# A depthwise convolution's taps in pairs, spread over three attention heads, and pooling one head ahead

## The chip, the cores and the metric

The kernel runs on one core of a Trainium2 chip. The metric is the time of one execution on the device in microseconds. The kernel before took 2637.24 us in the median of three runs (2633.56 to 2638.14).

## The reference, cut to what matters

Two networks of transformer blocks run one after the other on 512 latent tokens (x) and 256 context tokens, width 1024. The first network has two blocks, the second one. Only the mixing part of the first network's two blocks is touched. Each of these has three branches whose outputs are joined and projected: differential attention with 4 heads, a pooling of four window lengths, and a gated depthwise convolution over 31 tokens with a normalization behind it.

```python
for l in range(2):                     # the first network's two blocks
    ...
    attn = diff_attn_post(diff_attention(q, k_all, v_all, lam), subln_g[l], lambda_init)
    pool_o = pool_mixer(up, pool_w[l], pool_scale[l])
    conv_o = conformer_conv(ca, cb, conv_dw_w[l], conv_dw_b[l], conv_ln_g[l], conv_ln_b[l])
    mix = jnp.concatenate([attn, pool_o, conv_o], axis=-1)
    x = x + g1 * jnp.einsum('blm,md->bld', mix, w_out[l])
    ...                                # the first block does the same for the context tokens

def diff_attention(...):               # per 128 queries and head: two score maps
    p = jax.nn.softmax(s, axis=-1)
    a = p[:, :, 0] - lam * p[:, :, 1]  # the combination
    return jnp.einsum('bhqk,bhkd->bhqd', a.astype(v_all.dtype), v_all)

def multiscale_pool(u):                # mean of 2, 4, 8 or 16 neighbours, minus u
    ...
def conformer_conv(a, b, dw_w, dw_b, ln_g, ln_b):
    u = a * jax.nn.sigmoid(b)
    y = lax.conv_general_dilated(u, dw_w[:, None, :], ...)   # 31 taps on 256 channels
    return jax.nn.silu(layer_norm(y + dw_b, ln_g, ln_b))
```

## The kernel before

Activations lie with channels on the 128 partitions. Weights come in pieces of 512 KB by the SyncE queue and are split into a high and a low part, the high part on ScalarE (line 229), the low part on GpSimd (line 230); a projection is three matmuls for each product (lines 254, 257, 258).

**Attention.** `attn` goes through the four heads, and in each through query tiles of 128 rows: 6 tiles in the first block (two of the context, with 256 keys, and four latent ones with 768), 4 in the second. A tile's scores are matmuls into two PSUM tiles (line 836; the pool has two of them, so the next tile's scores wait until this tile's exponentials have read them). VectorE takes the row maximum (line 799), ScalarE the exponential (803), VectorE the reciprocal and lambda's factor (841 to 843) and the *combination* of the two maps (844). `attn_values`, for the tile before, transposes the combined map on TensorE (815), copies it on ScalarE (817), multiplies with the values (819), and normalizes with a power on GpSimd (297, tile `ray`) and two products on VectorE (860, 862); `turn` transposes the result (867).

**Work beside the heads.** `windows` returns five lists of items: one for the time before head 0, and one for each head, of which `layer` issues a share after each tile. Items are projections (`q1` and so on: each head's queries and keys are projected a head ahead, normalized on VectorE and GpSimd in `qk_norm`, lines 759 to 782, and turned on TensorE, 791), modulation columns (`m`), taps (`t`), pooling (`pool`), and the convolution's normalization (`ln`). An item's later stages wait in a list until enough matmul time has been issued.

**Convolution.** `conv_taps` runs on VectorE. There are 2 channel tiles (ct) of 31 taps each; a tap is one instruction over the whole token range (783 columns in the first block, 512 in the second) that multiplies a shifted view of `uc[ct]` by a column and adds it to the output tile `mix[6 + ct]` (line 664; the first one, with the bias, is line 662). Items hold four taps. Seven items stand in head 0's list and nine in head 1's. They are issued with a priority lowered by 1500 places. `conv_ln` (lines 671 to 690) takes means by a matmul with ones (676) and normalizes.

**Pooling.** `pool_mix` adds shifted views on GpSimd (line 614), two or four adds for each segment, into two scratch tiles, which are the convolution's inputs `uc`; so it can begin only when the taps have read these. VectorE does edges and the mean minus u (lines 639 to 644), a matmul the weights (649). Its two items stand in head 2's list, with the normalization.

**What sets the order.** The code is recorded in this order, and a scheduler then places instructions on each engine by priority (the place in the recording, raised or lowered by `high_priority`) along a timeline of its own. On the chip each engine runs its own list in that order, and waits by semaphores where it needs another engine's result.

## Time and profile before

| | us |
|---|---|
| median of 3 runs (lowest, highest) | 2637.24 (2633.56, 2638.14) |
| the profiled execution | 2634.79 |
| its span, first to last instruction | 2632.9 |
| TensorE busy | 2500.2 (95%) |
| VectorE busy | 954.6 (36%) |
| ScalarE busy | 907.7 (34%) |
| GpSimd busy | 1143.8 (43%) |

The busy shares are of the whole span, and the change touches two stretches of it: the attention of the first block, about 80 to 385 us, and that of the second, about 1100 to 1340 us. In the profile PE is TensorE, DVE VectorE, ACT ScalarE, POOL GpSimd. The granted clock of TensorE is given as a share of 2.4 GHz; at its lower level it is 1.2 GHz, so a stretch in which it is low for a fifth of the time shows 0.9. Times in views by time are from the span's start.

### The profile page before, as it was taken

To read this page: it belongs to the slowest core of one execution; us is meant where nothing else is said; L and a number is where in the kernel's file an instruction comes from. 1 tells how busy PE (TensorE), PEld (TensorE's weight loads), DVE (VectorE), ACT (ScalarE), POOL (GpSimd) and SP (SyncE) were. 2 spreads that over 40 slices of the span, in tenths; PEclk is the share of its full clock that TensorE was granted. 3 is DMA by queue.
4 is the path that set the end of the run, shared out by engine and by line. 5 is a ranking of instruction groups with operands and counts; after the bars stand their busy time and mean duration, and the time that the engine had idled before them with its cause. 6 is when DMAs were issued, how large, how long until landed. Compare 5 with 4: busy or idle time off the path is not lost.

```text
span 2632.9 us, 38646 instructions
## 1 busy us (share of the span) xinstructions
PE 2500.2 (95%) x15840; PEld 2131.1 (81%) x15840; DVE 954.6 (36%) x1932; ACT 907.7 (34%) x1905; POOL 1143.8 (43%) x965
## 2 busy tenths in 40 slices
PE   7889989999999999999999999999998898999998
PEld 5778869988888889877788777778887788888887
DVE  4896464121120123488542112113322756210112
ACT  4334543322122124333534223234443543422222
POOL 4544324433333334655326545454322344555553
PEclk9889989999999999999999999999998999999999
DMA  7113311323323233222324435343111021222221
GB/s 253 50 49 110 116 72 40 121 81 113 96 96 102 91 99 101 78 65 81 97 80 145 160 128 160 120 160 104 49 33 51 17 97 49 81 96 97 96 92 53
DMA packets 68961, 248.55 MB, mean 94 GB/s; under 512 B 7472, under 2 KB 10800, under 8 KB 67120
## 3 DMA queue, kind: packets, MB, share of 16 engines
q1 hardware_dynamic: 64992, 231.11, 26.9%
q10 hardware_dynamic: 3792, 14.97, 1.5%
q8 instruction: 125, 2.05, 0.3%
q14 instruction: 52, 0.43, 0.0%
HBM read 239.75 MB, written 6.29 MB: 93 GB/s over the span
## 4 chain that ended last, share of the span: by engine, by line
PE 48%; DVE 5%; ACT 2%; POOL 2%; issue 1%; DMA 1%; POOLq 0%; DVEq 0%; ACTq 0%
PE s2t L254 6%; PE s2t L258 6%; PE s2t L257 6%; PE pj L254 5%; PE pj L257 5%; PE pj L258 5%; PE ap L819 2%; DVE mix L664 1%; PE ap L254 1%; PE ap L257 1%; PE ap L258 1%; POOL wlo L230 1%; PE s2t L1531 1%; PE s2t L836 1%; PE ap L343 1%
## 5 line engine op out<-in xcount | busy, mean ns | idle before, releaser
L230 POOL TENSOR_TENSOR wlo<-raw,whi 128x512 fp32r<-128x512 f32 x576 | 745.4, 1326 | 700.5 <-ACT whi L229 700.2
L229 ACT CAST whi<-raw 128x512 fp32r<-128x512 f32 x576 | 319.5, 615 | 675.2 <-PE pj L257 248.1
L254 PE MATMUL s2t<-hh,whi 128*128 128x512 f32 (+1 forms) x1184 | 448.9, 380 | 0.8 <-ACT whi L229 0.8
L257 PE MATMUL s2t<-hl,whi 128*128 128x512 f32 (+1 forms) x1184 | 446.2, 377 | 1.8 <-POOL hl L428 1.8
L258 PE MATMUL s2t<-hh,wlo 128*128 128x512 f32 (+1 forms) x1184 | 447.5, 378 | 0.1
L254 PE MATMUL pj<-hh,whi 128*128 128x256 f32 (+1 forms) x1088 | 337.2, 312 | 8.5 <-ACT hh L425 2.9
L257 PE MATMUL pj<-hl,whi 128*128 128x256 f32 (+1 forms) x1088 | 331.5, 305 | 3.5 <-DVE hl L430 2.4
L258 PE MATMUL pj<-hh,wlo 128*128 128x256 f32 (+1 forms) x1088 | 331.1, 305 | 0.3 <-POOL wlo L230 0.3
L954 DVE TENSOR_TENSOR sg<-sg,s2t 128x512 f32<-128x512 f32 x66 | 45.4, 688 | 651.8 <-ACT sg L953 651.8
L257 PEld LDWEIGHTS s2t<-hl,whi 128*128 128x128 f32 x1184 | 223.0, 189 | 47.0 <-POOL hl L428 2.9
L258 PEld LDWEIGHTS s2t<-hh,wlo 128*128 128x128 f32 x1184 | 223.1, 188 | 46.9 <-issue 1.2
L254 PEld LDWEIGHTS s2t<-hh,whi 128*128 128x128 f32 x1184 | 222.4, 188 | 46.3 <-issue 2.1
L254 PEld LDWEIGHTS pj<-hh,whi 128*128 128x128 f32 x1088 | 210.4, 194 | 25.1 <-ACT hh L425 4.0
L327 POOL TENSOR_TENSOR gl<-sg,gh 128x512 fp32r<-128x512 f32 (+1 forms) x66 | 97.7, 1481 | 293.4 <-ACT gh L326 293.4
L257 PEld LDWEIGHTS pj<-hl,whi 128*128 128x128 f32 x1088 | 211.0, 194 | 12.4 <-DVE hl L430 2.6
L258 PEld LDWEIGHTS pj<-hh,wlo 128*128 128x128 f32 x1088 | 209.6, 193 | 8.5 <-POOL wlo L230 0.5
L254 PE MATMUL pj<-whi,hh 128*128 128x256 f32 x672 | 196.9, 293 | 1.3 <-ACT v L699 0.9
L257 PE MATMUL pj<-wlo,hh 128*128 128x256 f32 x672 | 194.4, 289 | 0.0
L258 PE MATMUL pj<-whi,hl 128*128 128x256 f32 x672 | 193.9, 289 | 0.0
L893 DVE SCALAR_TENSOR_TENSOR xt<-pj,mod,xt 128x256 f32<-128x256 f32 x224 | 101.6, 480 | 175.6 <-PE pj L258 175.1
L258 PE MATMUL pj<-gh,wlo 128*128 128x512 f32 (+1 forms) x400 | 145.6, 364 | 0.0
L254 PE MATMUL pj<-gh,whi 128*128 128x512 f32 (+1 forms) x400 | 145.5, 366 | 0.0
(382 smaller groups left out, 4464.7 us busy)
## 6 DMA issues: line engine op xcount, KB each, us to landing
raw<-in_w_mod SPq DMA_DIRECT2D x144, 512.0 KB, 4.0
raw<-in_w_up SPq DMA_DIRECT2D x132, 512.0 KB, 3.9
raw<-in_w_dn SPq DMA_DIRECT2D x66, 512.0 KB, 4.0
raw<-in_w_in SPq DMA_DIRECT2D x60, 512.0 KB, 3.9
raw<-in_w_out SPq DMA_DIRECT2D x24, 512.0 KB, 3.9
xt<-xs ACTq DMA_DIRECT2D x4, 1024.0 KB, 5.7
xt<-in_xT ACTq DMA_DIRECT2D x2, 1024.0 KB, 7.9
xs<-xt SPq DMA_DIRECT2D x2, 1024.0 KB, 3.8
```

Source lines behind the costliest of these rows:

```text
L229: nc.scalar.copy(out=h, in_=raw[:, q])
L230: nc.gpsimd.tensor_tensor(out=lo[:, s][:, q], in0=raw[:, q], in1=h.bitcast(F32), op=ALU.subtract)
L254: i = mm(ps, lhsT=lh, rhs=rh, start=start, stop=False)
L257: mm(ps, lhsT=lh, rhs=rl, start=False, stop=False)
L258: return mm(ps, lhsT=ll, rhs=rh, start=False, stop=stop)
L327: (lo_eng or self.nc.vector).tensor_tensor(out=lo, in0=src, in1=hi.bitcast(F32), op=ALU.subtract)
L343: nc.tensor.matmul(ps[g:g + 32], lhsT=self.cond_t[:, k, :], rhs=raw[k // 4][:, k % 4, :], start=k < 4, stop=k >= 4, tile_position=(0, g))
L664: nc.vector.scalar_tensor_tensor(out=m, in0=u[:, j:j + W], scalar=dw(j), in1=m, op0=ALU.mult, op1=ALU.add)
L819: i = nc.tensor.matmul(o, lhsT=at[:, j], rhs=v[:, j0 + j, :], start=j0 + j == 0, stop=j0 + j == nj - 1)
L836: nc.tensor.matmul(s[c][:, k0:k1], lhsT=qk[r, 0, a, t], rhs=qk[r, 1, b, k0:k1], start=n == 0, stop=n == 2)
L893: self.nc.vector.scalar_tensor_tensor(out=x, in0=ps, scalar=col, in1=x, op0=ALU.mult, op1=ALU.add)
L954: nc.vector.tensor_tensor(out=sg[:, c], in0=sg[:, c], in1=p[:, 1], op=ALU.mult)
```

## The change

Three things, in the items of `windows` and in what they issue:

- An item holds two taps in place of four. Of 32 items, 11 stand in head 0's list (22 taps), 10 in head 1's (19) and 11 in head 2's (21). The priority is lowered by 300 places in place of 1500.
- The first tap of an item is ordered behind the last combination recorded before it (`self.pace`). Both are on VectorE, so this is an order in its list and no wait for another engine.
- Pooling moves from head 2's list to head 1's, and its scratch is `mix[2]` and `mix[3]`, the outputs of heads 2 and 3. The normalization's items stand at the end of head 2's list and are no longer spread over it.

```diff
--- before.py
+++ after.py
@@ -27,6 +27,9 @@
 WINDOWS = (2, 4, 8, 16)
 TAPS = 31
 PAD = TAPS // 2
+TAPS_STEP = 2
+TAPS_LATER = 300
 CTX = slice(0, NCX)
 LAT = slice(NCX, NT)
 
@@ -608,7 +611,8 @@
 
         return c if self.CW == NX + NCX + PAD and c < NCX else (c + PAD if self.CW != NX else c - NCX)
 
-    def pool_mix(self, pa, l, ct):
+    def pool_mix(self, pa, l, ct, scratch):
 
         nc = self.nc
         add = lambda o, a, b: nc.gpsimd.tensor_tensor(out=o, in0=a, in1=b, op=ALU.add)
@@ -622,7 +626,7 @@
                 s = [None] * 4
                 prev, ln = u, L + 16
                 for i in range(2 if ct == 0 else 4):
-                    t = self.uc[i % 2]
+                    t = scratch[i % 2]
                     r = slice(64, 128) if i == 2 * ct + 1 else slice(0, 128)
                     st = 1 << i
                     ln -= st
@@ -653,15 +657,18 @@
 
     def conv_taps(self, pa, l, mix, ct, j0, j1):
 
         nc = self.nc
         W = self.CW
         m, u = mix[6 + ct][:, 0:W], self.uc[ct]
         dw = lambda j: self.DWH[:, ct * TAPS + j:ct * TAPS + j + 1]
         for j in range(j0, j1):
             if j == 0:
-                nc.vector.tensor_scalar(out=m, in0=u[:, 0:W], scalar1=dw(0), scalar2=self.pv(f"dwb{l}", ct), op0=ALU.mult, op1=ALU.add)
+                i = nc.vector.tensor_scalar(out=m, in0=u[:, 0:W], scalar1=dw(0), scalar2=self.pv(f"dwb{l}", ct), op0=ALU.mult, op1=ALU.add)
             else:
-                nc.vector.scalar_tensor_tensor(out=m, in0=u[:, j:j + W], scalar=dw(j), in1=m, op0=ALU.mult, op1=ALU.add)
+                i = nc.vector.scalar_tensor_tensor(out=m, in0=u[:, j:j + W], scalar=dw(j), in1=m, op0=ALU.mult, op1=ALU.add)
+            if j == j0 and self.pace is not None:
+                self.order(i, self.pace)
 
     def conv_ln(self, pa, l, mix, c, L):
 
@@ -719,7 +726,7 @@
         gr = ("0", "1", "2") if l == 0 else ("1", "2")
         fm = lambda n: [(n, ct, g) for ct in "01" for g in gr]
         tm = lambda n: [(n, g) for g in "012"]
-        taps = [("t", ct, j) for ct in "01" for j in range(0, TAPS, 4)]
+        taps = [("t", ct, j) for ct in "01" for j in range(0, TAPS, TAPS_STEP)]
         mod = lambda n: [("m",)] * n
 
         def merge(*ls):
@@ -740,9 +747,9 @@
         conv = [it for g in ("01", "2") for n in "gu" for it in fm(n) if it[2] in g]
         return [
             [("u", ct, "0") for ct in "01"] + q0 + v0 if l == 0 else q0[:2] + v0[:2] + q0[2:] + v0[2:] + conv,
-            merge(tm("q1") + fm("p"), taps[:7], mod(nm[0])),
-            merge(tm("q2") + tm("v1"), taps[7:], mod(nm[1])),
-            merge(tm("q3") + [("pool", 0), ("pool", 1)] + [("ln", g) for g in ((0, 1) if l == 0 else (1,))], mod(nm[2])),
+            merge(tm("q1") + fm("p"), taps[:11], mod(nm[0])),
+            merge(tm("q2") + tm("v1") + [("pool", 0), ("pool", 1)], taps[11:21], mod(nm[1])),
+            merge(tm("q3"), taps[21:], mod(nm[2])) + [("ln", g) for g in ((0, 1) if l == 0 else (1,))],
             [("sp", int(g), 0) for g in gr] + [("x",)] + mod(nm[3])
             + merge([("o", int(g), m) for g in gr for m in range(KD)], [("sp", int(g), 1) for g in gr]),
         ]
@@ -841,7 +848,7 @@
         nc.vector.reciprocal(out=w, in_=ss)
         nc.vector.tensor_copy(out=og["r0"][:, i:i + 1], in_=w[:, 0:1])
         nc.vector.scalar_tensor_tensor(out=w[:, 1:2], in0=ss[:, 0:1], scalar=self.LAM[l], in1=w[:, 1:2], op0=ALU.mult, op1=ALU.mult)
-        nc.vector.scalar_tensor_tensor(out=e[0][:, 0:nk], in0=e[1][:, 0:nk], scalar=w[:, 1:2], in1=e[0][:, 0:nk], op0=ALU.mult, op1=ALU.add)
+        self.pace = nc.vector.scalar_tensor_tensor(out=e[0][:, 0:nk], in0=e[1][:, 0:nk], scalar=w[:, 1:2], in1=e[0][:, 0:nk], op0=ALU.mult, op1=ALU.add)
         return e[0], nk
 
     def attn_values(self, pa, l, hd, g, i, e, nk, v, og, mix):
@@ -871,7 +878,7 @@
 
     def attn(self, pa, l, qk, v, mix, done):
 
-        prev = turn = None
+        prev = turn = self.pace = None
         for hd in range(4):
             for g in range(0 if l == 0 else 1, 3):
                 for i in range(2):
@@ -1053,11 +1060,11 @@
                         return self.mod_slot(*self.mods.pop(0))
                     if name == "t":
                         def taps():
-                            with self.tc.high_priority(-1500):
-                                self.conv_taps(pa, l, mix, int(it[1]), it[2], min(it[2] + 4, TAPS))
+                            with self.tc.high_priority(-TAPS_LATER):
+                                self.conv_taps(pa, l, mix, int(it[1]), it[2], min(it[2] + TAPS_STEP, TAPS))
                         return taps
                     if name == "pool":
-                        return self.pool_mix(pa, l, it[1])
+                        return self.pool_mix(pa, l, it[1], mix[2:4])
                     if name == "ln":
                         return self.conv_ln(pa, l, mix, (0, NCX)[it[1]], (NCX, NX)[it[1]])
                     if name == "x":
```

The same instructions are issued in both kernels; their order differs. The line numbers of the changed kernel are higher by 3 at the start and by 7 at the end of this part (a tap is line 669, the combination line 851, the row maximum line 806).

VectorE, first block, up to and just behind the first combination. `mix_173` and `mix_174` are the convolution's two output tiles, `ss`, `rsv`, `nm` and `qk` the next queries' normalization. Before:

```order
L841 RECIPROCAL rr<-sa 128x2
L664 SCALAR_TENSOR_TENSOR mix_174<-uc,DWH,mix_174 128x783
L779 TENSOR_TENSOR sq<-nm,sg 128x256 x2
L799 TENSOR_REDUCE nmx<-s2t 128x1
L664 SCALAR_TENSOR_TENSOR mix_173<-uc,DWH,mix_173 128x783
L799 TENSOR_REDUCE nmx<-s2t 128x1
L842 COPY r_1391<-rr 128x1
L843 SCALAR_TENSOR_TENSOR rr<-sa,lam_91,rr 128x1
L327 TENSOR_TENSOR qk<-pj,qk 128x2x256
L664 SCALAR_TENSOR_TENSOR mix_174<-uc,DWH,mix_174 128x783
L664 SCALAR_TENSOR_TENSOR mix_173<-uc,DWH,mix_173 128x783
L844 SCALAR_TENSOR_TENSOR e<-e,rr 128x256
```

Now:

```order
L299 TENSOR_SCALAR rsv<-ss 128x8
L772 TENSOR_TENSOR nm<-y,rsy 128x512
L786 TENSOR_TENSOR sq<-nm,sg 128x256 x2
L330 TENSOR_TENSOR qk<-pj,qk 128x2x256
L769 TENSOR_REDUCE ss<-sq 128x8
L806 TENSOR_REDUCE nmx<-s2t 128x1 x2
L299 TENSOR_SCALAR rsv<-ss 128x8
L848 RECIPROCAL rr<-sa 128x2
L849 COPY r_1391<-rr 128x1
L850 SCALAR_TENSOR_TENSOR rr<-sa,lam_91,rr 128x1
L851 SCALAR_TENSOR_TENSOR e<-e,rr 128x256
L669 SCALAR_TENSOR_TENSOR mix_173<-uc,DWH,mix_173 128x783 x2
```

A tap stood between each two steps of the chain; now the chain stands by itself up to the combination, and two taps of one tile come behind it.

VectorE, second block, from the fourth combination of that block on. `mix_10044` and `mix_10045` are the two output tiles there. Before:

```order
L844 SCALAR_TENSOR_TENSOR e<-e,rr 128x768
L664 SCALAR_TENSOR_TENSOR mix_10045<-uc,DWH,mix_10045 128x512
L765 TENSOR_TENSOR nm<-y,rsy 128x512
L762 TENSOR_REDUCE ss<-sq 128x8
L664 SCALAR_TENSOR_TENSOR mix_10044<-uc,DWH,mix_10044 128x512
L664 SCALAR_TENSOR_TENSOR mix_10045<-uc,DWH,mix_10045 128x512
L296 TENSOR_SCALAR rsv<-ss 128x8
L664 SCALAR_TENSOR_TENSOR mix_10044<-uc,DWH,mix_10044 128x512
L664 SCALAR_TENSOR_TENSOR mix_10045<-uc,DWH,mix_10045 128x512
L664 SCALAR_TENSOR_TENSOR mix_10044<-uc,DWH,mix_10044 128x512
L664 SCALAR_TENSOR_TENSOR mix_10045<-uc,DWH,mix_10045 128x512
L765 TENSOR_TENSOR nm<-y,rsy 128x512
```

Now:

```order
L851 SCALAR_TENSOR_TENSOR e<-e,rr 128x768
L869 TENSOR_TENSOR on<-ap,ray 128x256
L669 SCALAR_TENSOR_TENSOR mix_10044<-uc,DWH,mix_10044 128x512
L772 TENSOR_TENSOR nm<-y,rsy 128x512
L769 TENSOR_REDUCE ss<-sq 128x8
L669 SCALAR_TENSOR_TENSOR mix_10044<-uc,DWH,mix_10044 128x512
L299 TENSOR_SCALAR rsv<-ss 128x8
L669 SCALAR_TENSOR_TENSOR mix_10044<-uc,DWH,mix_10044 128x512 x3
L772 TENSOR_TENSOR nm<-y,rsy 128x512
L669 SCALAR_TENSOR_TENSOR mix_10044<-uc,DWH,mix_10044 128x512
L786 TENSOR_TENSOR sq<-nm,sg 128x256 x2
L669 SCALAR_TENSOR_TENSOR mix_10044<-uc,DWH,mix_10044 128x512 x2
```

The first rows are alike; before, the run of taps goes on to 35 up to the next combination, now there are 9, all of the first tile.

GpSimd, first block, where pooling begins. `up_175` is its input, `wlo` are weight splits. Before:

```order
L297 TENSOR_TENSOR rsy<-rsv,mhalf 128x8
L777 TENSOR_TENSOR y<-nm,cg 128x512
L782 TENSOR_TENSOR y<-y,sq 128x512
L614 TENSOR_TENSOR uc<-up_175 128x271
L614 TENSOR_TENSOR uc<-uc 64x269
L297 TENSOR_TENSOR ray<-rav,mhalf 128x2
L614 TENSOR_TENSOR uc<-up_175 128x527
L614 TENSOR_TENSOR uc<-uc 64x525
```

Now:

```order
L300 TENSOR_TENSOR rsy<-rsv,mhalf 128x8
L233 TENSOR_TENSOR wlo<-raw,whi 128x512 x2
L618 TENSOR_TENSOR mix_171<-up_175 128x271
L233 TENSOR_TENSOR wlo<-raw,whi 128x512 x2
L784 TENSOR_TENSOR y<-nm,cg 128x512
L618 TENSOR_TENSOR mix_172<-mix_171 64x269
L789 TENSOR_TENSOR y<-y,sq 128x512
L300 TENSOR_TENSOR ray<-rav,mhalf 128x2
L618 TENSOR_TENSOR mix_171<-up_175 128x527
L618 TENSOR_TENSOR mix_172<-mix_171 64x525
```

The adds begin ahead of the two query products (`y`) behind which they began before, among the same weight splits, and write `mix` tiles where they wrote `uc`.

## Rows read from the trace of the kernel before

**Rows 1.** Page, part 1, then part 2: busy tenths in 40 slices of 65.8 us.
```profile
PE 2500.2 (95%) x15840; PEld 2131.1 (81%) x15840; DVE 954.6 (36%) x1932; ACT 907.7 (34%) x1905; POOL 1143.8 (43%) x965
...
PE   7889989999999999999999999999998898999998
...
DVE  4896464121120123488542112113322756210112
...
PEclk9889989999999999999999999999998999999999
```

**Rows 2.** Stretches: length, busy per engine (instructions), granted clock, DMA share, GB/s.
```profile
80.00:220.00 140.00, 121.81 (x839) 107.85 (x838) 125.36 (x192) 44.66 (x112) 69.81 (x46) 0.87 0.19 60
220.00:320.00 100.00, 100.00 (x849) 85.66 (x848) 58.98 (x143) 46.64 (x118) 40.99 (x35) 1.00 0.39 128
320.00:350.00 30.00, 22.21 (x127) 17.25 (x126) 20.41 (x45) 14.91 (x41) 14.57 (x12) 0.77 0.16 50
350.00:380.00 30.00, 23.49 (x155) 19.90 (x154) 23.43 (x61) 19.37 (x54) 3.48 (x2) 0.94 0.27 106
1130.00:1240.00 110.00, 97.55 (x702) 82.49 (x701) 103.33 (x171) 39.36 (x92) 62.83 (x43) 0.94 0.21 67
1240.00:1300.00 60.00, 59.68 (x476) 50.12 (x474) 28.40 (x58) 27.04 (x65) 19.38 (x16) 1.00 0.27 91
1300.00:1360.00 60.00, 50.18 (x372) 44.38 (x371) 32.12 (x75) 28.64 (x70) 13.59 (x13) 0.98 0.30 106
```

**Rows 3.** The same view for the taps' line alone.
```profile
80.00:220.00 140.00, 73.27 (x60) 0.87 0.19 60
...
1124.00:1240.00 116.00, 50.65 (x60) 0.94 0.23 72
```

**Rows 4.** VectorE in order of time: start, length, line, operation, tiles, shapes, count.
```profile
81.33 2.10 DVE L664 SCALAR_TENSOR_TENSOR mix<-uc,DWH,mix 128x783 f32<-128x783 f32 x2
...
93.71 0.68 DVE L762 TENSOR_REDUCE ss<-sq 128x8 f32<-128x512 f32 x1
94.30 1.97 DVE L664 SCALAR_TENSOR_TENSOR mix<-uc,DWH,mix 128x783 f32<-128x783 f32 x2
96.19 0.16 DVE L296 TENSOR_SCALAR rsv<-ss 128x8 f32<-128x8 f32 x1
96.26 2.91 DVE L664 SCALAR_TENSOR_TENSOR mix<-uc,DWH,mix 128x783 f32<-128x783 f32 x3
...
99.69 0.68 DVE L765 TENSOR_TENSOR nm<-y,rsy 128x512 f32<-128x512 f32 x1
```

**Rows 5.** TensorE in order of time; in brackets idle before, and what ended it.
```profile
101.96 0.33 PE L791 MATMUL pj<-ident,y 128*128 128x128 f32 x1 [2.72 <-POOL y L770]
...
120.45 1.47 PE L836 MATMUL s2t<-qk 64*128 64x256 f32 x6 [3.07 <-ACT e L803]
...
185.09 1.00 PE L836 MATMUL s2t<-qk 64*128 64x256 f32 x3 [2.62 <-ACT e L803]
...
336.10 0.66 PE L867 MATMUL ap<-ident,on 128*128 128x128 f32 x2 [5.72 <-DVE on L862]
...
1228.15 1.09 PE L791 MATMUL pj<-ident,y 128*128 128x128 f32 x4 [5.85 <-DVE mod L356]
```

**Rows 6.** VectorE in order of time, without taps, at head 3's begin.
```profile
319.63 0.69 DVE L765 TENSOR_TENSOR nm<-y,rsy 128x512 f32<-128x512 f32 x1 [1.75 <-POOL rsy L297]
...
323.63 0.17 DVE L841 RECIPROCAL rr<-sa 128x2 f32<-128x2 f32 x1 [0.76 <-ACT e L803]
```

**Rows 7.** Taps and pooling's adds, by line: duration ns min/median/max, first, last start.
```profile
L664 DVE SCALAR_TENSOR_TENSOR mix<-uc,DWH,mix x120: 724/1020/2122, 81.3 to 1207.7; 128x783 f32<-128x783 f32 x60, 128x512 f32<-128x512 f32 x60
...
L614 POOL TENSOR_TENSOR uc<-uc x12: 629/1061/1864, 197.0 to 1223.7; 64x525 f32<-64x525 f32 x2, 128x525 f32<-128x525 f32 x2, 128x521 f32<-128x521 f32 x2, 64x513 f32<-64x513 f32 x2
```

**Rows 8.** GpSimd in order of time, head 3.
```profile
330.38 3.02 POOL L230 TENSOR_TENSOR wlo<-raw,whi 128x512 fp32r<-128x512 f32 x2
333.37 0.87 POOL L297 TENSOR_TENSOR ray<-rav,mhalf 128x2 f32<-128x2 f32 x1
```

## The prediction

> **What bounds the kernel now.** I read the page's first two parts, then busy time by stretch, then TensorE's waits, then VectorE in order of time. The page shows TensorE busy for 95% of the span; after the start it dips in slices 2, 3 and 6, and in slices 2 and 3 VectorE stands at 8 and 9 tenths with TensorE's clock at 8 [rows 1]. So only time that TensorE loses can be won. I count two losses in a stretch: microseconds in which TensorE is idle, and half-rate time. A granted share of 0.87 means that 0.13 of the stretch's pulses are missing; of these I charge the part that falls in busy time.
>
> - First block, heads 0 and 1 (80 to 220 us): idle 140 − 121.81 = 18.2; pulses 0.13 × 140 × 0.87 (the busy share) = 15.8. Lost: 34.0. VectorE is busy 125.36 of 140, and 60 taps (73.27 us, 1.22 each) are all in there [rows 2, 3].
> - First block, head 2 (220 to 320 us), no tap left: TensorE loses nothing at a granted 1.00, VectorE is busy 58.98 of 100 [rows 2].
> - Head 3 and its end: 320 to 350 loses 7.8 + 0.23 × 30 × 0.74 = 12.9; 350 to 380 loses 6.5 + 1.4 = 7.9.
> - Second block, 1130 to 1240 us: 12.4 + 0.06 × 110 × 0.89 = 18.3 lost, VectorE busy 103.33 of 110; 1240 to 1300: 0.3; 1300 to 1360: 9.8 + 1.0 = 10.8 [rows 2].
>
> How taps do it stands in VectorE's order of time: between the reduction that a head's normalization begins with (93.71) and the product that ends it (99.69) stand five taps, 1.97 and 2.91 us; TensorE then waits 2.72 us for the turned queries that hang on it [rows 4, 5]. The waits of 3.07 and 2.62 us at 120.45 and 185.09 are for an exponential on ScalarE, which frees the score bank and itself needs VectorE's row maximum [rows 5]. The granted clock falls to its lower level, 1.2 GHz, behind such waits and costs nearly as much again [rows 2].
>
> **The change part by part.** No instruction is added or taken away; the orders differ only between about 80 and 440 us and between 1125 and 1390 us of the run before, but for a few matmuls near 2250. So everything else I leave at its time.
>
> *Taps later.* Counted in the two orders of VectorE: up to the first combination of the first block stood 32 taps and now stand 4; up to the sixth 60 and now 22. 38 taps × 1.22 = 46 us leave the road of the first six tiles. In the second block 35 taps stood between the fourth and the fifth combination, now 9 do: 26 × 0.84 (50.65/60, [rows 3]) = 22 us. That takes away the cause of the waits above. But it isn't free: the taps go into head 2, where VectorE now has air. From 80 to 320 us it works 125.4 + 59.0 = 184.3 us. If TensorE lost nothing that stretch would take 240 − 34 = 206 us, and VectorE would be busy for 89% of it, not for 77%. The 22 us left over are 18 tiles × 1.2 us, and a tile's chain stops VectorE by itself: 1.75 us behind GpSimd's power, 0.76 us behind an exponential [rows 6], where nothing is put into the hole. So I don't credit all 34. Ends: 0 (VectorE stays the bound) and 34 (its waits are all filled by taps). The nearest row is 220 to 320, where 59% cost TensorE nothing; at 89% I take 20, a little over half. Likewise 1130 to 1300: 103.3 + 28.4 = 131.7 us of VectorE in 170 − 18.3 − 0.3 = 151.4, 87%; I credit 11 of 18.3, ends 0 and 18.
>
> *The ordering behind a combination.* It makes no semaphore between engines: both stand on VectorE. What is queued behind a pair of taps is the next tile's row maximum, and ScalarE's exponential and TensorE's score bank wait for that. A pair costs 2 × 1.22 = 2.4 us at most; the next tile's scores mostly come later than that, which is the cover. Where it is gone the price is in the third rival.
>
> *One tile at a time.* Before, taps of the two channel tiles alternated (three took 2.91 us, 0.97 each); now a pair works on one tile, each tap on the result of the one in front. Two such at 81.33 took 2.10, 1.05 each [rows 4]. The new order has 16 such neighbours in the first block and 15 in the second: 31 × 0.08 = 2.5 us of VectorE, hidden by the same air as the other taps; 2.5 us if none of it were.
>
> *Pooling a head ahead.* Its adds no longer wait for the last tap to free the scratch, and stand about where they stood between GpSimd's weight splits. In the second block its edges and the last taps kept VectorE full around the 5.85 us wait at 1228.15, which a VectorE reduction ended [rows 5]; that wait is in the 18.3. The new scratch belongs to heads 2 and 3, whose outputs are written later: no wait, and at worst one add, 1.06 us in the median [rows 7].
>
> *Normalization at the end of head 2's list.* Its matmuls still come in head 3. The 5.72 us wait at 336.10 is for a product that waited for GpSimd's power, which stood behind two weight splits of 3.02 us [rows 5, 8]: no tap is in it. The new order has head 3 looser and pooling out of it; of 12.9 I credit 3 (ends −5 and 13). The 7.9 and 10.8 at the blocks' ends are chains without other work: 0.
>
> Sum: −20 − 11 − 3 = −34 on the profiled execution's 2634.79 (span 2632.9 and 1.9 around it): 2600.8, say 2601. The median of the runs is 2.4 above it and inside their spread, so I add nothing.
>
> **A rule that speaks against it.** Taps lasted 724 to 2122 ns, and pooling's second and later adds 629 to 1864 [rows 7]: the two engines hold each other up. The Trainium skill, page "SBUF — State Buffer", section "Who interferes with whom", says that a VectorE instruction with two SBUF inputs contends with a GpSimd one that reads SBUF, and that the loser is blocked for the other's whole length rather than slowed. The spread of the rows bears that out. By it, the 12 adds of the first block, which ran after the taps and now run among them, would each cost a tap up to an add. That would be the second rival. The rows alone give its price: 12 × 1.06 = 13 us of VectorE, more than half of its air. I hold it for the less likely case, since an add meets a tap only when both are up.
>
> **Rivals.**
> 1. *All comes back.* The chain is covered everywhere, as in 220 to 320 now. For it: each tile's scores stand several microseconds of other matmuls ahead of their transposes. Against it: 89% on VectorE. −34 − 18.3 − 12.9 = −65: 2570. Chance 0.15.
> 2. *VectorE becomes the bound of heads 1 and 2.* Each of the 18 tiles stops it once behind a power and once behind an exponential, and each of the 12 adds blocks a tap: 184.3 + 18 × 2.51 + 13 = 242 us, as long as the 240 of today, so nothing is won there. In the second block some 10 tiles and 6 adds make 131.7 + 25 + 6 = 163 of 170: 7 won. With head 3's 3: −10, 2625. For it: the 89%. Against it: the order puts taps into most of these holes. Chance 0.18.
> 3. *Slower: taps come between scores and their row maximum in a stretch that has no loss today.* 40 of the 62 taps now follow the sixth combination; if each of them lands ahead of a row maximum that TensorE's bank waits for, 40 × 1.22 = 49 us go onto the path against the 34 won in heads 0 and 1, and in the second block 22 us of moved taps stand against 18 won: +49 − 34 + 4 = +19, before any half-rate time: 2654. It decides once VectorE's share of head 2 reaches 1: 59 + 40 × 1.22 = 108 us in 100 if all of them fell there. Against it: a third of them falls in head 1's end, and pooling leaves. Chance 0.08.
> 4. *It moves and gives back.* What heads 0 and 1 win is lost in heads 2 and 3: 2634, within 0.2%. Chance 0.06.
> Forecast: 0.53, own range 2586 to 2616.
>
> **How the numbers follow.** 0.2% is 5.3 us, about what a measurement of this kernel can tell from no change. Faster: 0.53 + 0.15 + 0.18 = 0.86; same 0.06; slower 0.08. The range reaches down to near the first rival's 2570 and up over the second's: 2572 to 2634; left out are 0.08 of the third, half of the fourth, and a little of the first.
>
> **What would show it.** Right: 80 to 200 us of the first block at a granted 0.95 or more, the first combination some 15 us sooner; taps in all of 80 to 290; VectorE near 85 to 90% there; the last tile's combination 15 to 30 us sooner, and the second block shorter by 8 to 15. The wait at 1228 gone. Wrong: TensorE waiting for exponentials in heads 1 and 2 with taps in front of the row maximum (third rival), or a combination that comes no sooner at the end of head 2 although it does at the end of head 0 (second). The 5.72 us wait of head 3 should be there in some size. If the first six tiles are not sooner at all, taps were not what held them, and the whole sum is wrong.

## The result, and the profile after

The changed kernel takes 2653.26 us (median of 6 runs, 2649.49 to 2658.62), the one before 2637.69 us in the same series. The ratio is 1.0059, 95% interval 1.0037 to 1.0081: slower by 0.6%, where 2601 us was predicted. The profiled execution spans 2654.6 us, 21.7 more than before.

The page of the kernel after, part 1 and then part 2, which answers [rows 1]:

```profile
PE 2521.7 (95%) x15840; PEld 2141.3 (81%) x15840; DVE 959.4 (36%) x1932; ACT 909.2 (34%) x1905; POOL 1138.3 (43%) x965
...
PE   7998989999999999999889999999998899999998
...
DVE  4497764121120223487553111113321756210112
...
PEclk9998989999999999988999999999998999999999
```

Read the first line beside the span. TensorE's idle time is 2654.6 − 2521.7 = 132.9 us; before it was 2632.9 − 2500.2 = 132.7. Of the 21.7 us, 21.5 are *busy* time, for the same 15840 matmuls. Over the whole span the change did not make TensorE wait longer, it made its work last longer. The busy share is 95% in both and shows nothing of it.

Four stretches of [rows 2], kernel after (length, busy of TensorE, weight loads, VectorE, ScalarE, GpSimd with counts, granted clock, DMA share, GB/s):

```profile
80.00:220.00 140.00, 131.99 (x1000) 116.08 (x999) 108.21 (x206) 53.45 (x134) 71.50 (x55) 0.96 0.22 70
220.00:320.00 100.00, 87.87 (x638) 71.71 (x638) 70.94 (x126) 38.70 (x99) 32.67 (x24) 0.91 0.32 108
320.00:350.00 30.00, 22.30 (x140) 18.20 (x140) 21.40 (x42) 14.01 (x40) 15.65 (x12) 0.83 0.16 51
1130.00:1240.00 110.00, 106.51 (x660) 86.23 (x659) 85.61 (x151) 38.29 (x88) 54.07 (x38) 0.84 0.20 62
```

By the prediction's own count (idle, plus missing pulses in busy time) 80 to 220 us now loses 8.0 + 0.04 × 140 × 0.94 = 13.3 instead of 34.0: 20.7 won, as forecast. But 220 to 320 loses 12.1 + 0.09 × 100 × 0.88 = 20.0 where it lost nothing. And 1130 to 1240 has TensorE busy for 106.5 of 110 us, 9 more than before, and finishes 660 matmuls, 42 fewer. VectorE, relieved as planned, is at 85.6 instead of 103.3.

The combinations on VectorE show the same along the way. In the first block the first one ends at 104.0 us instead of 130.9, the sixth 20.8 us sooner, the tenth 21.5 sooner (206.7), the fourteenth 6.9 *later*, and the last 5.8 later (374.2). The second block begins 1.6 later and ends 21.2 later (1350.4 for 1329.3).

Cut at these combinations, the stretches hold nearly the same work, and busy and idle time can be compared. First the first block from the sixth combination to the last, then the second block up to its last, each time the kernel before and the kernel after:

```profile
185.60:368.40 182.80, 171.73 (x1313) 145.35 (x1312) 119.86 (x287) 86.94 (x230) 72.42 (x62) 0.93 0.29 95
164.80:374.20 209.40, 180.45 (x1308) 149.18 (x1307) 169.92 (x343) 93.11 (x244) 83.12 (x64) 0.93 0.28 93
...
1093.00:1329.30 236.30, 217.00 (x1614) 184.81 (x1614) 173.95 (x309) 103.71 (x240) 109.62 (x80) 0.97 0.26 85
1095.00:1350.40 255.40, 236.23 (x1611) 196.61 (x1609) 175.58 (x308) 103.62 (x237) 108.92 (x79) 0.91 0.24 79
```

The two blocks lose differently. In the first, TensorE needs 26.6 us more behind the sixth combination: its idle time goes from 11.1 to 29.0 us, and its busy time grows by 8.7. The equal sum of idle time over the whole span hides this, since from 80 us up to the sixth combination it falls from 16.7 to 3.3. In the second block idle time stays (19.3 and 19.2 us), and all 19 us are busy time.

Two places show what happens. First the second block, TensorE in order of time, kernel after (start, length, line, operation, tiles, rows × columns of the weights, shape):

```profile
1143.28 0.58 PE L261 MATMUL pj<-whi,hl 128*128 128x256 f32 x1
1143.79 0.58 PE L843 MATMUL s2t<-qk 64*128 64x256 f32 x1
1144.30 0.58 PE L257 MATMUL pj<-whi,hh 128*128 128x256 f32 x1
1144.81 0.58 PE L843 MATMUL s2t<-qk 64*128 64x256 f32 x1
...
1150.42 0.41 PE L260 MATMUL pj<-wlo,hh 128*128 128x256 f32 x1
1150.64 0.41 PE L261 MATMUL pj<-whi,hl 128*128 128x256 f32 x1
```

Score matmuls (64 rows, L843) and projection matmuls (128 rows) take turns one by one, and start 0.51 us apart. When the turns end, at the same lower clock, projections of the same size start 0.22 us apart. No bracket stands behind any of these rows: nothing is waited for. The stretches show that the clock falls there as well, and that no other engine is full. The first row is the kernel before, the others the kernel after:

```profile
1140.00:1150.00 10.00, 10.00 (x61) 7.88 (x60) 8.38 (x15) 3.68 (x9) 1.27 (x2) 1.00 0.01 2
...
1140.00:1150.00 10.00, 10.00 (x25) 5.80 (x25) 4.46 (x7) 0.48 (x1) 0.00 (x0) 0.54 0.11 37
1210.00:1220.00 10.00, 10.00 (x51) 8.18 (x51) 6.88 (x13) 3.82 (x8) 4.95 (x5) 0.71 0.00 0
1220.00:1230.00 10.00, 10.00 (x31) 6.43 (x32) 4.72 (x6) 0.36 (x3) 3.20 (x2) 0.63 0.00 0
```

"Busy 10.00" with 25 matmuls in 10 us: the column of counts, not the busy time, tells it (the kernel before has 61 there, at a granted 1.00). A *turn* or *change* below is a place in TensorE's order where a score matmul follows another kind or the other way round. From a block's first score to its last I count 102 and 92 of them in the two blocks before, 110 and 132 after.

Second, head 2 of the first block, kernel after: TensorE, ScalarE, VectorE and GpSimd in order of time (in brackets idle before, and what ended it):

```profile
251.80 1.01 PE L843 MATMUL s2t<-qk 64*128 64x256 f32 x3 [6.16 <-ACT e L810]
...
251.18 0.47 ACT L810 ACTIVATE e<-s2t,nmx 128x256 f32<-128x256 f32 x1 [5.41 <-DVE nmx L806]
...
245.28 2.04 DVE L669 SCALAR_TENSOR_TENSOR mix<-uc,DWH,mix 128x783 f32<-128x783 f32 x1
247.24 1.22 DVE L299 TENSOR_SCALAR rav<-ss 128x2 f32<-128x2 f32 x1
248.37 2.11 DVE L669 SCALAR_TENSOR_TENSOR mix<-uc,DWH,mix 128x783 f32<-128x783 f32 x1
250.41 0.74 DVE L806 TENSOR_REDUCE nmx<-s2t 128x1 f32<-128x256 f32 x2
...
241.84 4.65 POOL L233 TENSOR_TENSOR wlo<-raw,whi 128x512 fp32r<-128x512 f32 x3
246.45 1.99 POOL L789 TENSOR_TENSOR y<-y,sq 128x512 f32<-128x512 f32 x1
248.40 1.26 POOL L233 TENSOR_TENSOR wlo<-raw,whi 128x512 fp32r<-128x512 f32 x1
```

This is the third rival as written: two taps, each of 2.0 to 2.1 us with GpSimd at work beside them (1.02 is the median in [rows 7]), stand between a tile's scores and its row maximum, and TensorE waits 6.16 us for the bank. The profile shows both suspects, so the experiments had to tell them apart.

### The profile page after: what moved, and what is told of

It is laid out like the page before. It is cut to its first block, busy times and chain, and to the rows that moved or that the text cites. A ratio compares the mean times of both kernels' runs of the same rounds, so it can differ in the third digit from the quotient of the medians.

```text
span 2654.6 us, 38640 instructions
## 1 busy us (share of the span) xinstructions
PE 2521.7 (95%) x15840; PEld 2141.3 (81%) x15840; DVE 959.4 (36%) x1932; ACT 909.2 (34%) x1905; POOL 1138.3 (43%) x965
## 4 chain that ended last, share of the span: by engine, by line
PE 49%; DVE 3%; POOL 2%; ACT 2%; issue 1%; DMA 1%; POOLq 0%; DVEq 0%; ACTq 0%
PE s2t L257 6%; PE s2t L261 6%; PE s2t L260 6%; PE pj L257 6%; PE pj L261 6%; PE pj L260 5%; PE ap L826 2%; POOL wlo L233 1%; PE s2t L843 1%; PE ap L257 1%; PE ap L260 1%; PE ap L261 1%; PE s2t L1538 1%; PE ap L346 1%; PE ap L822 1%
## 5 line engine op out<-in xcount | busy, mean ns | idle before, releaser
L257 PEld LDWEIGHTS pj<-hh,whi 128*128 128x128 f32 x1088 | 207.8, 191 | 26.1 <-ACT hh L428 3.9
```

What stands on the lines that cost most here:

```text
L257: i = mm(ps, lhsT=lh, rhs=rh, start=start, stop=False)
```

## The experiments

Three theories follow. Theory 1: scores and projections that take turns one by one make TensorE's work longer and let its clock fall. Theory 2: taps ordered behind combinations hold VectorE up in the second block. Theory 3: taps in front of row maxima cost the first block its gain. Ratios are against the kernel before on the same chip, with 95% intervals.

### Halves of the change

**Taps without the pooling.** Pooling goes back to head 2 and to the convolution's buffers as scratch; it then overwrites what the last taps still read, so this kernel computes something else there.

```diff
-merge(tm("q2") + tm("v1") + [("pool", 0), ("pool", 1)], taps[11:21], mod(nm[1])),
+merge(tm("q2") + tm("v1"), taps[11:21], mod(nm[1])),
-merge(tm("q3"), taps[21:], mod(nm[2])) + [("ln", ...
+merge(tm("q3") + [("pool", 0), ("pool", 1)], taps[21:], mod(nm[2])) + [("ln", ...
-return self.pool_mix(pa, l, it[1], mix[2:4])
+return self.pool_mix(pa, l, it[1], self.uc)
```

> The taps as changed (pairs, behind a combination, three heads); pooling stays in head 2 with the convolution's buffers as scratch, as before. In the built order the two blocks then have 118 and 90 changes between score matmuls and others on TensorE, against 102 and 92 before and 110 and 132 in the changed kernel. Theory 1 (the second block loses because projections and scores alternate one by one on TensorE, and that comes with pooling a head ahead): the second block is back at its time before or gains the 11 us that the prediction gave it, the first stays about as in the changed kernel (+3 us, its 20 us won in heads 0 and 1 and lost again in head 2): 2629 to 2644 us against 2638 before. Theory 2 (the second block loses because taps ordered behind a combination hold up VectorE): the second block stays 18 us behind, 2650 to 2656 us.

Measured 2630.30 us, 0.9981 [0.9969, 0.9993]. From its first combination to its last the second block, its taps spread as in the changed kernel, is some 8 us shorter than before. Theory 2 falls. The first block has won nothing here either: its last combination comes at 369.8 us, against 368.4 before, with 118 changes.

**Pooling without the taps**: taps in fours, unordered, at the old priority; pooling in head 1 with the new scratch.

> Only the pooling goes one head ahead with scratch of its own; the taps stand as before (fours, unordered, 32 of them in front of the first combination). 112 and 130 changes between scores and others on TensorE in the two blocks. Theory 1 (alternation, brought by the pooling): the second block is 12 to 18 us longer with the taps untouched, 2648 to 2656 us. Theory 2 (taps behind combinations): no change, 2634 to 2642 us.

Measured 2654.31 us, 1.0069 [1.0056, 1.0082]: 18 us slower with not one tap moved. Moving the pooling items regroups the list that says behind which tile each projection is handed out, and with 92 changes grown to 130 the second block's last combination comes 22 us later. That is busy time again: to that combination TensorE is busy 239.5 us for 1669 matmuls (from 1089 us), in the kernel before 217.0 us for 1614 (from 1093 us).

**One block at a time**, by making each edit depend on `l`.

> The whole change in the first attention block alone; the second has the order of before. Both theories: the combinations of heads 0 and 1 come some 20 us sooner, head 2 loses most of it again where its row maxima stand behind two taps of 2 us, end of the block at about +3 us: 2634 to 2644 us. If the second block's loss was a consequence of the first (a later start, other transfers, the clock it inherits), the whole +16 us stays: 2650 to 2656 us.

> The whole change in the second attention block alone; the first has the order of before. Both theories: the second block is 13 to 18 us longer by itself, 2650 to 2657 us, with half-clock stretches where TensorE shows about 25 to 50 matmuls in 10 us while it is busy all the time. If the loss hangs on the first block: 2634 to 2644 us.

Measured 2649.47 us, 1.0045 [1.0033, 1.0057], and 2649.58 us, 1.0050 [1.0038, 1.0062], the second within 1 us of its bounds. The second block's loss is its own, as both theories said. The first alone missed its bounds (2634 to 2644). Measured at the weight pieces' casts on ScalarE, its profile is 1 us late when the second block begins, 6 when that block, which is unchanged, has ended, and 15 behind other unchanged code, where 2010 to 2110 us has a granted clock of 0.76 against 0.86 before. So the halves don't add up (14 and 14 against 16 together). Several us can come that way in the profile of any kernel here, and only differences well above that are read from single stretches below.

### The same work with the scores in runs

Each projection matmul that stood alone or in a short group between the scores of one tile is ordered in front of that tile's first score. No engine, buffer or instruction changes.

```diff
+BEHIND = {11145: [10720], 11253: [10750, 10751, ...], ...}   # score: projections in front of it
+def tied(self, i):
+    n = int(i.ins.name[2:])
+    self.made[n] = i
+    for a in BEHIND.get(n, ()):
+        self.order(i, self.made[a])
+    return i
-        mm = self.nc.tensor.matmul
+        mm = lambda *a, **k: self.tied(self.nc.tensor.matmul(*a, **k))
...
-                        nc.tensor.matmul(s[c][:, k0:k1], ...)
+                        self.tied(nc.tensor.matmul(s[c][:, k0:k1], ...))
```

> The changed kernel with 45 projection matmuls of the second block, which stood one by one between the score matmuls of a tile, ordered in front of the tile's first score (or behind its last): 46 changes between scores and others on TensorE in that block instead of 132, same matmuls, same taps per tile, same pooling; the first block as in the changed kernel. Theory 1 (one-by-one alternation costs the second block its time, at about 0.2 us a change, and lets the clock fall): the second block gets back the 11 us of alternation and most of the 10 us of half clock and some more, since it has fewer changes than before the change: 2628 to 2640 us. Rival (the loss is VectorE's, which is late with row maxima and pooling work; alternation only fills the time): TensorE idles instead, 2648 to 2656 us. Second rival (scores start later because projections now go first, and the exponentials with them): 2656 to 2662 us.

Measured 2637.51 us, 1.0009 [0.9998, 1.0020]: 45 matmuls moved by a few places give 16 us back. The stretch 1090 to 1400 us, of the kernel after and of this one:

```profile
1090.00:1400.00 310.00, 285.52 (x2002) 244.55 (x2001) 191.09 (x342) 119.16 (x273) 124.91 (x95) 0.92 0.23 75
```

```profile
1090.00:1400.00 310.00, 276.81 (x2170) 249.46 (x2169) 207.08 (x371) 138.17 (x319) 144.15 (x116) 0.94 0.25 85
```

168 more matmuls in 9 us *less* of busy time. Idle time grew from 24.5 to 33.2: part of the turns had filled waits, so the rival of "no gain" was a little right.

> The kernel before with the same rule in the second block alone: 23 projection matmuls ordered in front of the tile's first score, 58 changes instead of 92. Theory 1: 34 changes at 0.15 to 0.2 us, 5 to 7 us less, 2629 to 2633 us. Rival (alternation only fills time in which TensorE would wait): no change, 2634 to 2640 us.

Measured 2639.53 us, 1.0020 [1.0008, 1.0031]: a miss for theory 1, slower by 5. In this kernel TensorE's idle time in the same stretch rises from 26.1 to 35.0 us (275.04 busy). VectorE is nearly full there [rows 2], so scores that come later behind other matmuls probably cost more than the turns did. Matmuls per busy us are 7.6 in both, so the 34 changes taken out can't be seen there, and the clock is at 0.94 for 0.97. Runs do not pay everywhere.

> The changed kernel with 62 projection matmuls of both blocks ordered in front of a tile's scores: 86 and 46 changes instead of 110 and 132; taps and pooling as changed. Theory 1 (alternation and the clock that falls with it took the first block's 20 us back as well): some 12 to 18 us less than with the second block alone ordered so (2637.5): 2619 to 2627 us. Theory 3 (the first block gave its gain back because taps stand in front of row maxima in head 2 and last 2 us beside GpSimd's splits): the wait of 6 us at 246 us and the half clock behind it stay, 2633 to 2640 us.

Measured 2622.60 us, 0.9953 [0.9939, 0.9967], 15 us less than with the second block alone, where theory 3 expected 2633 or more. But this run does not tell the two theories apart in the first block: no tap was moved, two taps of 2.0 and 2.1 us still stand in front of the row maximum there, and yet the wait of 6.16 us is gone (1.0 us is the longest for an exponential). The block's last combination comes at 355.3 us, 18.9 sooner than in the kernel after, but 10.7 of that are won up to the sixth, and behind it the block still takes 201.2 us, 24 of them idle. The versions with pooling in head 2, below, say more. The stretch 120 to 130 us, kernel after, then this one:

```profile
120.00:130.00 10.00, 10.00 (x52) 7.66 (x51) 1.82 (x2) 2.81 (x7) 1.79 (x2) 0.85 0.00 0
```

```profile
120.00:130.00 10.00, 10.00 (x88) 9.27 (x86) 8.30 (x13) 5.19 (x12) 5.68 (x5) 1.00 0.33 107
```

The kernel after was losing busy time inside the very stretch where the prediction saw its gain, and there was more to gain: the sixth combination comes at 154.1 instead of 164.8.

### Taps in front of row maxima

```diff
-nc.vector.tensor_reduce(out=nm, ..., op=ALU.max, negate=True)
+self.pace = nc.vector.tensor_reduce(out=nm, ..., op=ALU.max, negate=True)
-self.pace = nc.vector.scalar_tensor_tensor(out=e[0]...
+nc.vector.scalar_tensor_tensor(out=e[0]...
```

> The changed kernel with each pair of taps ordered behind the row maximum made last, instead of behind the last combination; fours of switches nearly as there (114 and 130 changes). Theory 3 (taps in front of row maxima): the wait of 6 us at 246 us goes, the first block ends 8 to 15 us sooner, 2638 to 2646 us. Theory 1 (alternation): the waits move, the time stays: 2648 to 2657 us.

Measured 2659.29 us, 1.0095 [1.0080, 1.0110], above the bounds of both theories. TensorE's waits of this kernel, 195 to 412 us (in all, times, longest):

```profile
PE ap L874 <- DVE on L869: 4.9, 1, 4.9
PE pj L798 <- POOL y L777: 4.0, 1, 4.0
PE pj L798 <- POOL y L789: 3.7, 1, 3.7
PE pj L257 <- DVE xc L900: 3.7, 1, 3.7
PE s2t L843 <- ACT e L810: 3.5, 3, 1.3
```

The 6.16 us wait for an exponential is gone (1.3 is the longest left), and waits for turned queries stand in its place. Theory 3 names a real wait, and taking the taps away from it in this way wins nothing.

### The price by itself

Behind the last output of the kernel before, chained matmuls of 256 columns (`0` and `1` the two halves of 64 rows, `2` and `3` all 128):

```diff
+put(*[2, 2] * 96); put(*[0, 1] * 48); put(*[2, 3] * 48)
+put(*[0, 2, 1, 2] * 96); put(*[2, 2] * 96)
+put(*[0, 1, 0, 1, 0, 1, 2, 2, 2, 2, 2, 2] * 16)
+put(*[0, 2] * 96); put(*[2, 2] * 48)
```

> The kernel before, with 1440 more matmuls of 256 columns chained behind the last output on TensorE, in this order: 192 with all 128 rows; 96 with 64 rows, the halves in turn; 96 with 128 rows into two banks in turn; 384 in which one of 64 rows and one of 128 take turns; 192 with 128 rows; 192 in turns of six and six; 192 in turns of one and one with the same half; 96 with 128 rows. Theory 1: the groups of one kind take 0.11 to 0.12 us a matmul, the turns of one 0.20 to 0.31 us, with the granted clock falling to half in the 384 although TensorE never waits; the turns of six lie at about 0.14 us. Rival (the change of rows costs nothing, the attention's matmuls wait for something else): 0.12 us in all of them at full clock.

The stretches, in the order of that list without the last (columns as above):

```profile
2636.00:2660.00 24.00, 24.00 (x187) 24.00 (x187) 0.00 (x0) 0.00 (x0) 0.00 (x0) 0.92 0.05 16
2661.00:2666.00 5.00, 5.00 (x88) 5.00 (x86) 0.00 (x0) 0.00 (x0) 0.00 (x0) 1.00 0.02 3
2667.00:2678.00 11.00, 11.00 (x94) 11.00 (x93) 0.00 (x0) 0.00 (x0) 0.00 (x0) 1.00 0.01 1
2690.00:2870.00 180.00, 180.00 (x355) 100.93 (x354) 0.00 (x0) 0.00 (x0) 0.00 (x0) 0.50 0.00 0
2871.00:2894.00 23.00, 23.00 (x177) 23.00 (x177) 0.00 (x0) 0.00 (x0) 0.00 (x0) 0.91 0.00 1
2896.00:2918.00 22.00, 22.00 (x186) 17.85 (x182) 0.00 (x0) 0.00 (x0) 0.00 (x0) 1.00 0.01 1
2930.00:3013.00 83.00, 83.00 (x164) 46.61 (x163) 0.00 (x0) 0.00 (x0) 0.00 (x0) 0.50 0.00 0
```

Measured in one run with a profile. One kind: 11/94 = 0.12 us a matmul. The two halves in turn: 5/88 = 0.06, they run beside each other. Turns of one: 180/355 = 0.51 us at half clock; before the clock fell they started 0.31 apart (2678.34, 2678.65, 2678.97 in the trace), 0.19 more than one kind. Turns of six and six: 22/186 = 0.12 on average, at full clock. That looks like no price, but half of these matmuls are halves, which by themselves take 0.06:

```profile
2900.03 0.63 PE L1689 MATMUL s2t<-pw,pa 64*128 64x256 f32 x6
2900.59 0.97 PE L1691 MATMUL pj<-pw,pa 128*128 128x256 f32 x6
2901.49 0.62 PE L1689 MATMUL s2t<-pw,pa 64*128 64x256 f32 x6
```

Twelve take 1.46 us (2900.03 to 2901.49), where 6 × 0.06 + 6 × 0.12 = 1.08 would do without changes. The 0.38 over are two changes at 0.19 each, the price of the turns of one. So a change costs 0.19 us in both orders; sixes have fewer of them for each matmul, and the clock stayed up. The kernels' own attention shows the same: at full clock 256-column matmuls of one kind start 0.12 us apart, and one that stands alone between two of the other kind takes 0.31 (medians of the kernel after).

By this price, as an estimate, the 40 changes more of the second block (132 for 92) are 7.6 of the 19 us that it lost. The rest can lie in the clock: at 0.91 for 0.97 some 16 us of pulses more are missing in it.

### What the taps are worth, and a faster kernel

Pooling in head 2 again, its scratch now the fourth head's output tile and one new tile, so that the output stays what it was:

```diff
+spare = pmix.tile([128, NX + 16], F32, name="spare")
-return self.pool_mix(pa, l, it[1], mix[2:4])
+return self.pool_mix(pa, l, it[1], (mix[3], spare))
```

> The taps as changed, pooling in head 2 as before but with scratch of its own (the fourth head's output tile and one new tile), so that neither side waits for the other's buffer: 122 and 90 changes. Theory 1 (pooling's earlier place brought the alternation): the second block gains some 7 us as when the pooling stood back on the convolution's buffers, the first block gives its 20 us back: 2626 to 2634 us. If that earlier result came from the shared buffers: 2638 to 2650 us.

Measured 2634.19 us, 0.9997 [0.9983, 1.0011]: the second block keeps its gain, the first gives its 20 us back, with no pooling in head 1. Both were forecast, and the time stands at the upper end of the range. With 122 changes this version has more turns in the first block than any other.

> The previous kernel with 43 projection matmuls of both blocks ordered in front of a tile's scores: 86 and 50 changes instead of 122 and 90. Theory 1: 76 changes at 0.12 to 0.2 us, 9 to 15 us less than the previous one: 2612 to 2624 us. Rival (alternation only fills waits): the same as the previous one, 2626 to 2634 us.

Measured 2611.83 us, 0.9910 [0.9896, 0.9925]: the fastest here, 23 us under the kernel before. Its page, parts 1 and 2, and its stretch 80 to 220:

```profile
PE 2476.8 (95%) x15840; PEld 2116.3 (81%) x15840; DVE 946.0 (36%) x1932; ACT 908.4 (35%) x1905; POOL 1135.9 (44%) x965
...
PE   7999889999999999988999999999998898999998
```

```profile
80.00:220.00 140.00, 131.57 (x1073) 117.21 (x1072) 115.98 (x225) 57.70 (x146) 73.60 (x58) 1.00 0.25 84
```

Its idle time is 2608.6 − 2476.8 = 131.8 us, once more that of before; what went is busy time. The stretch finishes 1073 matmuls where before finished 839 [rows 2].

> The kernel before (taps in fours, 32 of them in front of the first combination; pooling in head 2) with 34 projection matmuls of both blocks ordered in front of a tile's scores: 74 and 58 changes instead of 102 and 92. If runs and taps pay only together (TensorE still waits for the first exponentials in heads 0 and 1, where the prediction saw 18 us of idle time): 2630 to 2640 us. If the runs alone made the fastest version fast: 2608 to 2618 us.

Measured 2630.01 us, 0.9990 [0.9977, 1.0003]. So runs without the taps are worth at most 6 us, taps without the runs nothing that can be measured (2634.19), and both 23. In the profiles, block by block, the two come closer to a plain sum. The first block's last combination comes 13, 3 and 18 us sooner than before (at 355.5, 365.7 and 350.4), and the second block, from its first combination to its last, is 5 us longer, 10 shorter and 7 shorter. So it is not shown that they pay only together.

This version also answers what took the first block's gain. From the sixth combination to the last, first this kernel, then the two with the taps moved, without and with the scores in runs:

```profile
180.50:355.50 175.00, 164.81 (x1313) 141.57 (x1313) 115.14 (x286) 86.51 (x228) 65.82 (x59) 0.95 0.29 95
```

```profile
165.80:365.70 199.90, 179.23 (x1308) 147.75 (x1307) 157.64 (x327) 88.97 (x233) 80.82 (x64) 0.92 0.27 90
```

```profile
154.70:350.40 195.70, 169.61 (x1315) 141.94 (x1313) 161.00 (x336) 92.28 (x243) 81.75 (x64) 0.96 0.28 95
```

With the scores in runs in both, the version with the taps moved still takes 20.7 us longer there, and 16 of these are idle time (26.1 against 10.2). So turns cost some busy time, but most of the first block's gain went into waits, beside a VectorE that is busy for 161 instead of 115 us. The waits are of several kinds. In the fastest kernel the largest are 8.8 us for attention outputs from VectorE, 4.1 for turned queries, 2.9 for the combined maps' copies on ScalarE, 2.8 for queries from ScalarE, 2.3 for exponentials. That the taps cause them is likely, not shown: these two versions also differ in the pooling's scratch and in the place of the normalization.

> The taps as changed, pooling in head 2 with scratch of its own, scores in runs in the first block alone: 86 and 90 changes. If the runs pay in the first block only, as the profiles say (the second block of the fastest version is 7 us shorter than before, without runs 10 us): 2607 to 2614 us. If they pay in both: 2617 to 2624 us.

Measured 2613.24 us, 0.9916 [0.9898, 0.9934]: the runs pay in the first block. Those of the second add nothing clear here (2611.83 with both).

> The fastest so far (taps as changed, pooling in head 2 with scratch of its own, scores ordered in runs; 2611.8 us) with the taps behind the last row maximum instead of the last combination: 76 and 54 changes. If theories 1 and 3 both hold in part, the six-us waits of head 2 go and it gains another 3 to 8 us: 2603 to 2609 us. If taps in front of row maxima cost nothing once the scores stand in runs: 2609 to 2616 us.

Measured 2619.55 us, 0.9947 [0.9930, 0.9965], above both forecasts and slower than with the combination as the mark. Perhaps a tap behind the row maximum stands in front of the next combination instead; no run shows which wait it is.

## Why the prediction was wrong, step by step

- **What bounds the kernel**: "only time that TensorE loses can be won", counted as idle time and half rate. Too narrow. A third loss, busy time stretched by changes between kinds of matmuls and by the clock that falls with them, is in neither. In the second block it is the whole loss (236.2 us busy for 217.0, and idle as before). Two terms of the sum failed: pooling, put at nothing, and the −20 of the first block.
- **Taps later, first block, −20**: right where it was looked for. 80 to 220 us wins 20.7, the granted clock is 0.96, the first combination came 27 us sooner where 15 were said. What failed is the cover behind it: VectorE's air in head 2 was to take the taps with 20 left as a net gain. From the sixth combination to the last the block took 26.6 us more than before, 17.9 of them idle, so that its end came 5.8 later. Pooling is not the main reason: with pooling back in head 2 this stretch is still 17 us longer than before (199.9 for 182.8), 10 of them idle. Nor are turns: with the scores in runs it is 20.7 longer with the taps than without. That the moved taps cause these waits is likely and not shown by itself.
- **Taps later, second block, −11**: about right for the taps alone (some 8 us, pooling left in head 2). With pooling moved the block lost 19.6 instead, for the reason in the next point.
- **"Pooling a head ahead ... no wait, and at worst one add, 1.06 us"**: the term that failed in the second block. It looked for the price where the moved instructions run, on GpSimd and VectorE. But the items share a list with the projections, so TensorE's order changed; alone the move costs 18 us, most of it in the second block. That the orders differ was in the prediction's text; what stands next to what on TensorE was not looked at.
- **The ordering behind a combination** and the third rival: its chance of 0.08 was for the right sign, and in the first block for half of the mechanism: TensorE does wait more behind the sixth combination, by 17.9 us, where it allowed for up to 49. But the wait it names, for the bank behind a row maximum, is 6.16 us of that; it goes when the taps are moved, and nothing is won, and it also goes when TensorE's order alone changes and the taps stay. And the second block's loss is of another kind. That its 2654 lies next to the measured 2653.26 is luck.
- **Second rival, VectorE the bound**: not as written. VectorE is at 71% in 220 to 320 us, so it is not full; but from the sixth combination on it is busy 170 us instead of 120, and TensorE's waits grow there.
- **Head 3, −3, and the tails, 0**: 320 to 350 us loses 7.7 + 3.8 = 11.5 against 12.9. The 5.85 us wait at 1228 is gone, as foretold; four waits for turned queries, 9.9 us together and 7.0 at the longest, came in the second block instead. The 5.72 us wait is there as 6.86:

```profile
343.99 0.66 PE L874 MATMUL ap<-ident,on 128*128 128x128 f32 x2 [6.86 <-DVE on L869]
```

- **The contention of taps and GpSimd**: borne out (2.04 and 2.11 us beside splits, 1.03 in the median of 80 to 220 us). How much of the first block's waits comes from it, no run shows.

Open: how much of the first block's waits behind the sixth combination hangs on the taps themselves; why 2010 to 2110 us, the same code, has a granted clock of 0.86 in one profile and 0.76 in another; and why pooling in head 1 still costs 11 us with the scores in runs and about as many changes (2622.6 against 2611.8; 86 and 46, 86 and 50). Of the 9 us between those two profiles 6 stand at the second block's last combination. Up to it TensorE is busy as long in both (205.8 us from 1076 us, 206.3 from 1073.4), and idle 4 us longer with pooling in head 1. So the turns are not all of what pooling costs: once they are out, waits cost some of it.

## What to carry to other kernels

Divide a stretch's matmuls by its busy time: a TensorE that is "busy 10.00" with a third of its usual count is losing time without waiting. Before you cost a moved item by its own engine, look at what the scheduler then puts between matmuls of different row counts on TensorE. Count the changes: here each cost 0.19 us at full clock, in turns of one and of six alike, and long rows of single turns cost the clock as well. Fewer changes pay where TensorE is not kept waiting for the scores by it; in the kernel before they did not pay. When a gain comes as forecast in one stretch and is gone by the next, cut both traces at the same piece of work and compare busy and idle time: here one block lost by waits and the other by TensorE's order, and the sums over the whole span showed neither.

## What the hardware showed

At full clock 256-column matmuls take 0.12 us one after the other with 128 rows, 0.06 when the two halves of 64 rows take turns, and 0.31 when 64 and 128 rows take turns: 2.6 times the first. The Trainium skill, page "TensorEngine Tiling (Array Packing)", section "Key Properties", says that changing the tiling mode drains the engine. These rows agree that a change costs time, and give the price: 0.19 us, in turns of one and of six. Unexpected was the clock: in 190 us of turns of one, with TensorE busy throughout and never waiting, the granted clock fell to its lower level and stayed there, which makes 0.51 us a matmul, over four times the 0.12 of turns of six, which ran at full clock.
